# A two-line change to a block kernel on one core: the chain of each recurrence step gets the scheduler's high priority

## The chip, the cores and the metric

The kernel runs on one core of a Trainium2 chip. The time is that of one execution on the device, in microseconds (us); for the kernel before it is the median of three runs. The engines are TensorE (PE; its weight loads are shown as PEld), VectorE (DVE), ScalarE (ACT), GpSimd (POOL) and SyncE (SP), which here only issues transfers. Each engine takes its instructions in the order in which the built program holds them.

## What is computed

One block of a diffusion backbone over 2048 latent tokens and 256 context tokens of width 1024. Half of the channels go through a recurrence in 8 heads of 64, run forward and backward over context and latent tokens; the other half through a short gated convolution. Their joint output, after a projection, feeds 16 SwiGLU experts, each of which picks 256 tokens. The recurrence, per head:

```
def step(s, inp):
    r_t, w_t, k_t, v_t, a_t, b_t = inp
    sa = einsum('bhvk,bhk->bhv', s, a_t)
    s = s * w_t[:, :, None, :] + sa[..., :, None] * b_t[:, :, None, :] + v_t[..., :, None] * k_t[:, :, None, :]
    return s, einsum('bhvk,bhk->bhv', s, r_t)
```

After it: `x = x + g1 * (concat([a_x, b_x]) @ w_out)`, an RMSNorm with modulation, the router's softmax, top-k per expert, the experts, and a final RMSNorm.

## The kernel before

The program has three parts: the first projection (`proj_phase`), the recurrence with everything that is run beside it (`wkv_phase`), and the experts (`moe_phase`). The change lies in the second.

The recurrence works on chunks of C = 64 tokens: 4 of context and 32 latent, so NS = 36 steps, in each of which direction d = 0 takes a chunk from the front and d = 1 one from the back. For a step s there is preparation that needs nothing of the state: `prep` (L733, loads and scaling, for two steps at a time), `front` (L774, the 64 x 64 products, L782, masked by L784), `solve` (L806, L818 and L820: a triangular solve on DVE over two steps, with its input and output through DRAM), `merge` (L827, L839 and L843, into the one PSUM tile `pm`) and `tokmaj` (L793, transposes L798, and the load of `uv`). Then comes `chain(s)` (L846), the part that needs the state of the step before: for both directions PE forms `wy` (L857 from the state `Sb`, L860), ACT copies it to `w` (L863), PE forms `pu` (L869), ACT copies it to `uv` (L870), PE forms `ps` (L877), DVE adds it to the running state (L883) and writes the new `Sb` (two L886), POOL keeps a scaled copy (L888); PE then completes `wy` (L895). Up to step 19 a latent step's output goes to DRAM (`Y`, L899). From step TURN = 20 on the other direction has already left its half there: `chain` takes a tile `oy`, loads that half from `Y` (L850, by the helper at L57) and DVE adds `wy` to it (two L902).

`wy0` and `wy1` have one PSUM buffer each. `oy` comes from the tag `ev`, five buffers that it shares with the fill's tiles: `cu`, `cb`, `cvt` and `adacc` of the convolution and conditioning, `ccv` of the convolution's output projection, `ogg` and `ovb` of the last part.

Fill is work that PE does beside the chain: `conv_gen` (projection and convolution, 1728 of its matmuls L262 in this stage, with 256 columns), `ada_gen` (conditioning), `conv_out_gen` (L985, 16 tiles of tokens of 24 matmuls with 512 columns; loads `cx`, L998, adds with L1008, stores to `X1`, L1009), and `out_gen` (also L985, 16 tiles; normalizes `oy`, transposes with L1073, adds with L1086, router logits with L1111). All of the fill's PSUM goes through one buffer, `pj`; only for its last tiles does `out_gen` use `pg`, `pm` and others besides.

What sets the order: the program is built with a scheduler that simulates a time line. An instruction's priority is its place in the program as written; of the instructions that are ready on an engine, the one with the lowest number goes first. A tile's buffer is handed out in the same way. As the loop at L933 is written, `chain(s)` comes behind the fill of step s - 1, and `ready(s + 1)` (which calls `merge` and `tokmaj`), `scale` (which calls `prep`), `begin(s + AHEAD)` (which calls `front` and `solve`) and `fill` come behind `chain(s)`.

Of the kernel before, what the change touches and what calls it, by code (L numbers as in the profile page):

```python
# [693 lines left out]
def wkv_phase(ctx_, tc, k, I, S, fill):  # L694
    nc = tc.nc
    with ExitStack() as ctx:
# [208 lines left out]
        def begin(s):  # L905
            if s < NS:
                front(s)
                if s % 2:
                    solve(s // 2)

        def ready(s):
            if s < NS:
                merge(s)
                for d in range(2):
                    tokmaj(s, d)

        def scale(n):
            if n < NS // 2:
                for d in range(2):
                    prep(2 * n, d)  # L920
# [10 lines left out]
        begin(4)  # L931
        ready(0)
        for s in range(NS):  # L933
            chain(s)
            ready(s + 1)
            if s % 2:
                scale((s + 5) // 2)
            begin(s + AHEAD)
            fill(75 // 20 + 1 if s < TURN else 100, s >= TURN)
            if s == TURN:  # L940
                fill(0, True)


def first_half(tc, k, I, S):
    with ExitStack() as ctx:
        shared_pools(ctx, tc, k)
        fill = filler(tc, k, I, S)
        proj_phase(ctx, tc, k, I, S, fill)
        wkv_phase(ctx, tc, k, I, S, fill)
# [708 lines left out]
```

## Time and profile before

| | |
|---|---|
| median of 3 runs | 3159.18 us (3146.18 to 3162.34) |
| profiled execution: its own time | 3142.96 us |
| profiled execution: span, first to last instruction | 3141.1 us |
| PE, DVE, ACT, POOL busy | 92%, 68%, 44%, 21% of the span |
| mean granted clock of PE | 0.93 |
| first projection, recurrence, top-k and experts | 0 to 632, 632 to 1900, 1900 to 3141 us |

Times in the rows are in us from the first instruction of the profiled execution. An instruction of PE is shown with its latency; matmuls overlap, so the cost of one in a series is the distance between two starts. "Clock" is the share of TensorE's full clock that was granted.

### The profile page before, as it was taken

Reading aid. Unit: us, or ns where it says so; the run is one execution under the profiler, and the core shown is the slowest. Engines: PE = TensorE matmul, PEld = TensorE weight load, DVE = VectorE, ACT = ScalarE, POOL = GpSimd, SP = SyncE. Lnnn points to the kernel's source line nnn. Section 1 sums busy time; section 2 is a strip of 40 time slices with the busy share of each in tenths; the row PEclk is TensorE's granted clock in tenths of the full one; section 3 lists DMA queues with packets and bytes.
Section 4 is the critical chain, followed back from the end, with each engine's and each line's share of the span. In section 5 each row is a group of like instructions: output and inputs, shape, how many; then the busy total and the mean of one; then the engine's idle time right before and its main releaser. Section 6 shows DMA issues by size and latency. Waiting matters only on the chain. (4 is left out here: it accounts for less than half of the span.)

```text
span 3141.1 us, 62585 instructions
## 1 busy us (share of the span) xinstructions
PE 2881.8 (92%) x24367; PEld 2612.9 (83%) x24367; DVE 2141.5 (68%) x4611; ACT 1385.0 (44%) x2279; POOL 667.4 (21%) x893
## 2 busy tenths in 40 slices
PE   6988989889999999999999994999999999999997
PEld 4877978878888888778888873998999899999886
DVE  7688687766666666667767646666666666666776
ACT  6556645423344443224445443444444444444453
POOL 0243242533333322112222121000000000000011
PEclk8989999977999999998788986999999999999998
DMA  6466555666666655766665551666666666666886
GB/s 248 144 201 193 178 175 170 201 170 152 154 169 165 173 141 162 204 176 169 164 151 143 124 165 47 201 219 205 188 204 204 195 197 208 207 203 206 267 285 228
DMA packets 408745, 577.43 MB, mean 184 GB/s; under 512 B 175864, under 2 KB 257912, under 8 KB 407424
## 3 DMA queue, kind: packets, MB, share of 16 engines
q1 hardware_dynamic: 397504, 533.58, 56.4%
q0 software_dynamic: 10656, 38.80, 5.3%
q8 instruction: 191, 3.13, 0.4%
q10 hardware_dynamic: 288, 1.05, 0.1%
q14 instruction: 106, 0.87, 0.1%
HBM read 444.73 MB, written 128.59 MB: 183 GB/s over the span
## 5 line engine op out<-in xcount | busy, mean ns | idle before, releaser
L129 ACT CAST wH<-wr 128x1024 fp32r<-128x1024 f32 (+1 forms) x592 | 528.9, 897 | 844.7 <-PE pg L1429 408.8
L134 DVE TENSOR_TENSOR wL<-wr,wH 128x1024 fp32r<-128x1024 f32 (+1 forms) x586 | 627.6, 1076 | 353.5 <-ACT wH L129 347.6
L1429 PE MATMUL pg<-xH,wH 128*128 128x256 f32 x2048 | 585.4, 286 | 15.8 <-ACT s L1433 15.8
L1429 PE MATMUL pg<-xL,wH 128*128 128x256 f32 x2048 | 576.2, 282 | 0.0
L1429 PE MATMUL pg<-xH,wL 128*128 128x256 f32 x2048 | 575.7, 281 | 0.0
L262 PE MATMUL pj<-hH,wH 128*128 128x256 f32 x1600 | 478.0, 299 | 25.5 <-ACT cu L671 7.4
L262 PE MATMUL pj<-hH,wL 128*128 128x256 f32 x1600 | 469.4, 294 | 23.6 <-DVE wL L134 22.6
L262 PE MATMUL pj<-hL,wH 128*128 128x256 f32 x1600 | 468.1, 293 | 1.4 <-DVE hL L134 1.1
L1429 PEld LDWEIGHTS pg<-xH,wH 128*128 128x128 f32 x2048 | 389.5, 190 | 17.9 <-ACT s L1433 16.5
L1429 PEld LDWEIGHTS pg<-xL,wH 128*128 128x128 f32 x2048 | 389.3, 190 | 1.5
L1429 PEld LDWEIGHTS pg<-xH,wL 128*128 128x128 f32 x2048 | 389.5, 190 | 0.0
L262 PEld LDWEIGHTS pj<-hH,wH 128*128 128x128 f32 x1600 | 318.4, 199 | 37.6 <-DVE cu L674 8.4
L262 PEld LDWEIGHTS pj<-hH,wL 128*128 128x128 f32 x1600 | 316.6, 198 | 30.9 <-DVE wL L134 28.9
L262 PEld LDWEIGHTS pj<-hL,wH 128*128 128x128 f32 x1600 | 318.5, 199 | 5.6 <-DVE hL L134 2.0
L1488 POOL DMA_INDIRECT ACC<-o,it x30 | 50.8, 1694 | 954.4 <-DVE o L1474 800.7
L1446 PE MATMUL pd<-wH,hL 128*128 128x512 f32 x512 | 201.9, 394 | 0.0
L1446 PE MATMUL pd<-wL,hH 128*128 128x512 f32 x512 | 201.9, 394 | 0.0
L1446 PE MATMUL pd<-wH,hH 128*128 128x512 f32 x512 | 199.9, 395 | 0.0
L818 DVE TENSOR_TENSOR x<-X,x 128x120 f32<-128x120 f32 (+12 forms) x540 | 157.8, 296 | 57.7 <-DMA X<-TI 46.0
L820 DVE TENSOR_TENSOR X<-X,x 128x120 f32<-128x120 f32 (+12 forms) x540 | 163.0, 305 | 12.3
L782 PE MATMUL pg<-ar,bk 64*128 64x128 f32 x1152 | 141.0, 323 | 17.1 <-DVE g L784 7.5
L782 PEld LDWEIGHTS pg<-ar,bk 64*128 64x128 f32 x1152 | 114.4, 215 | 33.7 <-issue 13.5
(428 smaller groups left out, 5456.9 us busy)
## 6 DMA issues: line engine op xcount, KB each, us to landing
wr<-in_w_gate_dram SPq DMA_DIRECT2D x128, 512.0 KB, 4.2
wr<-in_w_up_dram SPq DMA_DIRECT2D x128, 512.0 KB, 4.8
wr<-in_w_down_dram SPq DMA_DIRECT2D x128, 512.0 KB, 3.3
wr<-in_w_in_dram SPq DMA_DIRECT2D x208, 256.0 KB, 3.2
bk<-KBD SPq DMA_DIRECT2D x36, 512.0 KB, 5.6
ar<-NR SPq DMA_DIRECT2D x36, 512.0 KB, 5.9
adaw<-in_ada_b_dram SPq DMA_DIRECT2D x32, 512.0 KB, 3.7
inc<-C SPq DMA_DIRECT2D x36, 256.0 KB, 3.1
```

Source lines behind the costliest of these rows:

```text
L129: nc.scalar.copy(H_, src)
L134: (leng or nc.vector).tensor_tensor(L_, src, H_.bitcast(F32), op=OP.subtract)
L262: nc.tensor.matmul(ps, wa[:, kw, :], ha[:, kt, :], start=m == 0, stop=m == 3 * KT - 1)
L782: nc.tensor.matmul(pg[:, p], bk[rows, p], ar[rows, p], start=True, stop=True)
L818: nc.vector.tensor_tensor(tv, X[:, 0:r, t:t + 1].to_broadcast([128, r, m]), x[:, t:t + 1, t + 1:].to_broadcast([128, r, m]), op=OP.mult)
L820: nc.vector.tensor_tensor(X[:, 0:r, t + 1:], X[:, 0:r, t + 1:], tv, op=OP.add)
L1429: nc.tensor.matmul(ps, a[:, ws], b[:, kt], start=i == 0, stop=i == 23)
L1446: nc.tensor.matmul(po[2 * m + n], a[:, f, ms], b[:, ns], start=f == 0 and q == 0, stop=f == FB - 1 and q == 2)
L1488: nc.gpsimd.indirect_dma_start(out=S["ACC"], out_offset=bass.IndirectOffsetOnAxis(ap=ids[m][:, :1], axis=0), in_=o, in_offset=None, comput ...
```

## The change

Each call of `chain` in the loop over the steps is put under the scheduler's high priority: its instructions, on every engine and its transfers too, go ahead of all others that are ready at the same time. Nothing else is edited. Lines behind L934 move by one, so L985 of before is L986 in the orders of the changed program, L1008 is L1009, and L1086 is L1087.

```
@@ -931,7 +931,8 @@
         begin(4)
         ready(0)
         for s in range(NS):
-            chain(s)
+            with tc.high_priority():
+                chain(s)
             ready(s + 1)
             if s % 2:
                 scale((s + 5) // 2)
```

On PE, between the `ps` matmuls of step 1 and the start of step 2, the order was (a row is one matmul, xN is N of them in a row; 64x64 is what is written of one head):

```order
L877 MATMUL ps<-uv,bt 64x64 x8
L843 MATMUL pm<-g,tz 32x32 x11
L782 MATMUL pg<-ar,bk 128x128 x2
L798 MATMUL pbt<-ident,bk 128x128 x4
L782 MATMUL pg<-ar,bk 128x128 x5
L798 MATMUL pbt<-ident,bk 128x128 x4
L782 MATMUL pg<-ar,bk 128x128
L857 MATMUL wy_8600<-Sb_7129,ar 128x128 x4
L860 MATMUL wy_8600<-uv,g 64x64 x8
```

and at the same place it is now

```order
L262 MATMUL pj<-hH,wH 128x256
L877 MATMUL ps<-uv,bt 64x64 x8
L262 MATMUL pj<-hL,wH 128x256
L877 MATMUL ps<-uv,bt 64x64 x8
L843 MATMUL pm<-g,tz 32x32 x16
L798 MATMUL pbt<-ident,bk 128x128 x4
L262 MATMUL pj<-hH,wL 128x256
```

The fill's matmuls (L262) now stand between the chain's; 14 of them lie between these `ps` and the next L857.

On DVE, around the adds into `oy` of step 20 (`wy_16033` and `wy_16047` are that step's two `wy`), the order was

```order
L1008 TENSOR_TENSOR cx<-pj,cx 128x512 x2
L883 TENSOR_TENSOR sc<-ps,sc 128x256
L886 TENSOR_TENSOR Sb_7129<-sc,pc 64x4x64 x2
L883 TENSOR_TENSOR sc<-ps,sc 128x256
L902 TENSOR_TENSOR oy<-wy_16033,oy 64x512
L973 TENSOR_TENSOR wo<-wo,g1row 128x512 x2
L886 TENSOR_TENSOR Sb_7130<-sc,pc 64x4x64 x2
L1008 TENSOR_TENSOR cx<-pj,cx 128x512
L902 TENSOR_TENSOR oy<-wy_16047,oy 64x512
```

and is now

```order
L836 STREAM_TRANSPOSE tz<-g 32x512
L1009 TENSOR_TENSOR cx<-pj,cx 128x512 x2
L134 TENSOR_TENSOR caL<-ccv,caH 128x512
L1009 TENSOR_TENSOR cx<-pj,cx 128x512 x2
L134 TENSOR_TENSOR caL<-ccv,caH 128x512
L1009 TENSOR_TENSOR cx<-pj,cx 128x512 x2
L134 TENSOR_TENSOR caL<-ccv,caH 128x512
L1009 TENSOR_TENSOR cx<-pj,cx 128x512
L902 TENSOR_TENSOR oy<-wy_16047,oy 64x512
L902 TENSOR_TENSOR oy<-wy_16033,oy 64x512
```

The two L902 stood beside the state update of their own step; now they stand behind the adds of the convolution's output tiles, nine of which are complete by then.

On DVE behind the last L902 of the recurrence the order held six adds L1086, of three output tiles. It now holds twelve (L1087), of six; this piece of it comes soon after that L902 and did not stand behind it before:

```order
L134 TENSOR_TENSOR oaL<-pw,oaH 128x512
L1137 SCALAR_TENSOR_TENSOR lg<-pj,or_20157,bb 64x16 x2
L1087 TENSOR_TENSOR ox<-pj,ox 128x512 x2
L1096 TENSOR_SCALAR oss<-oss 128x1
L1099 RECIPROCAL or_20434<-or_20434 128x1
L134 TENSOR_TENSOR oaL<-pw,oaH 128x512
L1137 SCALAR_TENSOR_TENSOR lg<-pj,or_20434,bb 64x16 x2
```

More of the last part's work is left for the time after the recurrence.

## Rows read from the trace of the kernel before

**Rows 1.** The page: the span, and section 1 (busy us, share, instructions) for PE.
```profile
span 3141.1 us, 62585 instructions
...
PE 2881.8 (92%) x24367; PEld 2612.9 (83%) x24367; DVE 2141.5 (68%) x4611; ACT 1385.0 (44%) x2279; POOL 667.4 (21%) x893
```
**Rows 2.** Busy time by stretch: stretch and length, engines' busy us (instructions), clock, DMA share, GB/s.
```profile
632.00:734.00 102.00, 87.21 (x730) 80.41 (x729) 73.27 (x179) 32.96 (x56) 38.42 (x53) 0.77 0.62 154
734.00:787.00 53.00, 52.47 (x483) 47.39 (x483) 30.32 (x66) 18.65 (x30) 11.70 (x17) 0.65 0.66 162
787.00:1411.00 624.00, 586.07 (x6202) 525.79 (x6200) 413.05 (x938) 229.55 (x390) 172.44 (x239) 0.96 0.62 168
1411.00:1443.00 32.00, 32.00 (x326) 26.86 (x325) 22.47 (x69) 5.58 (x9) 1.36 (x3) 1.00 0.66 180
1443.00:1707.00 264.00, 256.27 (x2541) 222.94 (x2541) 185.92 (x587) 128.77 (x247) 70.40 (x92) 0.82 0.65 157
1707.00:1855.00 148.00, 143.12 (x1610) 123.59 (x1608) 89.12 (x346) 65.84 (x143) 19.88 (x24) 0.95 0.49 117
1855.00:1900.00 45.00, 34.77 (x160) 27.41 (x159) 21.70 (x81) 20.99 (x37) 18.98 (x45) 0.79 0.72 221
```
**Rows 3.** PE's waits from 632 to 1900: us in total, times, longest.
```profile
PE pu L869 <- ACT w L863: 12.4, 6, 4.6
...
PE ps L877 <- ACT uv L870: 5.1, 3, 2.7
PE pj L985 <- DVE cx L1008: 4.9, 5, 1.6
...
PE wy L860 <- DMA uv<-V: 2.0, 1, 2.0
...
PE pj L985 <- DVE lg L1136: 1.2, 1, 1.2
```
**Rows 4.** PE in order of time from 730 to 790: start, length, what, how many.
```profile
733.60 1.06 PE L857 MATMUL wy<-Sb,ar 128*128 128x128 f32 x8
...
736.74 1.14 PE L860 MATMUL wy<-uv,g 64*64 64x64 f32 x16
...
753.48 2.07 PE L857 MATMUL wy<-Sb,ar 128*128 128x128 f32 x8
...
782.37 0.28 PE L262 MATMUL pj<-hL,wH 128*128 128x256 f32 x1
782.49 0.28 PE L262 MATMUL pj<-hH,wL 128*128 128x256 f32 x1
```
**Rows 5.** Two stretches of 20 us, with the columns of rows 2.
```profile
740.00:760.00 20.00, 20.00 (x172) 17.55 (x169) 11.48 (x20) 8.56 (x14) 8.06 (x13) 0.52 0.98 233
...
1220.00:1240.00 20.00, 20.00 (x248) 18.95 (x246) 13.01 (x20) 9.34 (x15) 3.04 (x4) 1.00 0.51 146
```
**Rows 6.** PE in order of time from 1435 to 1525, as rows 4.
```profile
1435.41 0.40 PE L985 MATMUL pj<-woH,caH 128*128 128x512 f32 x1
1435.64 0.39 PE L985 MATMUL pj<-woL,caH 128*128 128x512 f32 x1
...
1486.65 0.65 PE L1073 MATMUL pj<-ident,ox 128*128 128x128 f32 x4
...
1492.96 1.86 PE L1111 MATMUL pj<-rt,oxt 128*128 128x16 f32 x16
```
**Rows 7.** Groups by line, 632 to 1900: shapes, count | busy us, mean ns | idle before, releaser.
```profile
L886 DVE TENSOR_TENSOR Sb<-sc,pc 64x256 f32<-64x256 f32 x140 | 69.6, 497 | 1.8
...
L870 ACT COPY uv<-pu 64x512 f32<-64x512 f32 x72 | 40.9, 575 | 63.7 <-PE pu L869 63.5
...
L1008 DVE TENSOR_TENSOR cx<-pj,cx 128x512 f32<-128x512 f32 x32 | 22.0, 689 | 32.6 <-PE pj L985 25.7 <-DMA g<-TO 4.6 <-DMA cx<-in_x_dram 2.1
```
**Rows 8.** Transfers issued from 1240 to 1860: count, KB each, median us to landing.
```profile
cx<-in_x_dram SPq DMA_DIRECT2D x16, 512.0 KB, 4.2
X<-cx SPq DMA_DIRECT2D x16, 512.0 KB, 4.3
```

More of the change, by code (lines that the diff above doesn't have):

```diff
@@ L933, in wkv_phase @@
         for s in range(NS):
-            chain(s)
+            with tc.high_priority():
+                chain(s)
             ready(s + 1)
```

## Prediction, made before the changed kernel was run

> **What bounds the kernel now.** I read the page first, then a table of stretches, then TensorE's own waits, then its instructions in order of time. On the page TensorE (PE) is busy for 92% of 3141.1 us [rows 1]. The change touches one stage, the recurrence, from the first L857 at 632 us to the router's last logits at 1900 us. In the table by stretch PE is busy for 586 of 624 us, 256 of 264 and 143 of 148 there; length less busy time, added over all seven rows, is 76 of 1268 us [rows 2]. The largest wait for the chain itself, for the copy of `w`, is 12.4 us in 6 waits [rows 3]. So the recurrence isn't held up by its serial chain: PE has other work almost all the time, and moving the chain forward can't save a long wait, because there is none.
>
> What is lost here is lost to the clock. Eight matmuls of L857 take 1.06 us at 733.60 and 2.07 us at 753.48 [rows 4]: the two levels, 2.4 and 1.2 GHz. From 740 to 760 us PE is busy without a gap and the granted clock is 0.52; from 1220 to 1240 us it is just as busy at 1.00 [rows 5]. In the first stretch PE ran only the chain and its preparation (64 to 128 columns, often on part of the array); in the second it also ran L262 and L985 (256 and 512 columns, "wide" below). From [rows 2], (1 - clock) x length is 19 us for 734 to 787, 25 for 787 to 1411, 48 for 1443 to 1707 and 7 for 1707 to 1855: 98 us of PE work.
>
> **What the change moves.** Each engine gets the same instructions, but for two more loads of an activation table on ScalarE (ACT); so no work goes away, and only waits, clock and overlap can change. To see where the chain now stands I walked PE's order of both programs with full-clock rates: 0.12 us from one L262 to the next and 16 of L860 in 1.14 [rows 4], 0.23 from one L985 to the next, 4 of L1073 in 0.65 and 16 of L1111 in 1.86 [rows 6], the other small shapes likewise. (The order counts one row where the trace has two matmuls of f32.) By these rates the stage is 1006 us of PE work in either program; it takes 1268.
>
> 1. *Chain ahead of fill, steps 4 to 19.* These 16 steps held 503 us of PE work and now hold 432: fill that stood ahead of a step now stands behind it. That alone is worth **0**, since the fill still has to run before 1900.
>
> 2. *The stop at step 20.* The `oy` tile of step 20 gets a buffer only after the `ccv` tiles that share its pool. In the new order on VectorE (DVE) both L902 of step 20 stand behind the adds of L1008 for many tiles; L902 reads `wy`, which has one buffer, so L857 of step 21 can't start before. In PE's order 72 us pass between the two steps, with 20 groups of 12 L985 (ten tiles) that all go through the one `pj` buffer. Of their 19 hand-overs 8 have a block of `pm` matmuls between them and 11 have nothing. A bare hand-over costs 4.9/5 = 1.0 us [rows 3]: 11 us. The `cx` tiles have two buffers; a load of 4.2 and a store of 4.3 [rows 8] with two groups of 2.8 and two adds of 0.69 [rows 7] make 15.5 us for a buffer, 7.8 per tile against 7.2 of PE order: 6 us if only that binds, and 17 with the hand-overs on top. I take **+14**; ends 0 (all hidden) and 25 (each load also waits its turn on SP).
>
> 3. *The tail.* Behind the last L895 the order now has 14 groups of 12 L985, seven tiles, where it had 6 groups, three tiles. A tile is 24 x 0.23 + 3 x 0.65 + 1.86 = 9.3 us of PE; four more are 37 us that are merely moved. But their hand-overs through `pj` were filled by chain matmuls and now aren't. Two of the four tiles go through `pj` six times each, two (which also use `pg`) three times: 18 hand-overs. The rows for such are 1.0 (L1008) and 1.2 (the read into `lg`) [rows 3]: 18 to 22 us, less what of the next tile fits in. I take **+19**; ends 10 and 30.
>
> 4. *Shorter cover.* Between a step's last `pu` matmul and its first `ps` matmul the order now has 2.9 us of other PE work (median) where it had 3.9; between `ps` and the next L857 6.7 where it had 10.8. What must fit in is an ACT copy of 0.58 us, or on DVE an add and two products of 0.50 [rows 7]. Of the gaps ahead of `pu` and `ps` 38 were under 2.65 us, now 43; under 3.2 us 50, now 68. PE waited there 12.4 + 5.1 us in 9 waits [rows 3], some 0.4 us for each short gap; 5 to 18 more make 2 to 7 us. I take **+5**; ends 0 and 72 (the second rival below).
>
> 5. *Clock.* Wide matmuls now stand between chain matmuls more often. Stretches of PE order of 15 us and over without a wide one were 13 with 237 us, now 9 with 161; of 12 us and over, 15 with 265 us, now 15 with 239. The 98 us go with them: 0.41 us per us by the first count, 0.37 by the second, so the gain is 31 or 10 us. I take **-20**, between the two.
>
> 6. *Queues.* The chain's stores (L899) and loads of `oy` (L57) move forward on SP too, ahead of loads for the fill. PE's rows show 2.0 us for one late load of `uv` [rows 3] and no wait for weights, so these loads run ahead, and I cost it at **0**; if that cover went, a load that is late costs some 2 us each time, within the end of term 4.
>
> The sum is 14 + 19 + 5 - 20 = +18 us on the 3142.96 us of the profiled execution. That execution is 16 us under the median of the runs, 3159.18, so on the median I say **3177 us**. A measurement of this kernel can tell about 0.5%, 16 us, from no change.
>
> A rule of the skill bears on term 5. [rows 5] show half clock in 20 us in which PE had no gap. The Trainium skill, "TensorE: Matmul & The Clock Gate", section "HAM oscillation — how this bites in real kernels", ties the fall to TensorE waiting for data between bursts of matmuls. The trace disagrees with that as the whole story, since the clock was down without a wait; by that rule alone term 5 would be nothing and the sum +38.
>
> **The rivals.** *Faster by the clock.* Place: the stretches 734 to 787 and 1443 to 1707. If the mixing lifts the clock there to the 0.96 of 787 to 1411 [rows 2], 16 + 37 = 53 us come back in place of 20, and with terms 2 and 3 near their low ends (3 and 10) and term 4 at 4 the sum is 3 + 10 + 4 - 53 = -36: 3123. For it: the long stretches without wide matmuls do shrink. Against: steps 22 to 35 have some 24 to 36 L985 each, hardly more than the 24 before, and ten stretches of 11 us or more remain there. It decides from a mean clock over 0.94 in the stage up to the last step.
>
> *Chain at the head of the line.* PE takes its instructions in order. If ACT and DVE come later than the order supposes, every `pu` and `ps` group blocks the fill behind it. With a third of the 142 gaps at 1.5 us (the longest rows are 4.6 and 2.7 [rows 3]), term 4 is 72 in place of 5: 3159 + 85 = 3244. For it: the gaps are now all near their median. Against: gaps of that size rarely cost anything before.
>
> *Order is neutral.* What the stop and the tail cost, better mixing returns: 8 + 12 + 5 - 25 = 0, 3159.
>
> *The clock falls only where PE waits.* Then mixing gives nothing and terms 2 to 4 stand: +38, 3197. [rows 5] speak against it. The section of the Trainium skill named above describes this case.
>
> That the change doesn't do what it says is ruled out: the orders differ from step 0 on.
>
> **How the numbers follow.** My forecast has 0.46, of which 0.34 lies over 0.5% slower and 0.12 within; neutral 0.20; faster by the clock 0.22; head of the line 0.06; clock by waits alone 0.06. Slower by over 0.5%: 0.34 + 0.06 + 0.06 = 0.46. Within: 0.12 + 0.20 = 0.32. Faster: 0.22. The forecast's own range is 3159 to 3199 (terms 2 and 3 at 5 and 10, then at 25 and 30, the rest as taken). The whole range reaches down to 3115, which takes in most of the faster case, and up to 3225; the head of the line and the far end of the faster case, some 0.14, are left out.
>
> **What would show it.** Right: the stage is 10 to 35 us longer; a stretch of 75 to 95 us with hardly anything but L985 on PE, and waits of L985 for L1008 of 10 us or more; 90 to 110 us between the last L895 and the router's end, where it was 45; a clock over 0.82 in the steps after 21. Wrong: a clock of 0.95 throughout with a shorter stage (the first rival), or waits of PE for `w`, `uv` and `Sb` over 40 us (the second). If the part from 1900 on changes by over 5 us, something moved that I have not seen.

## The result, and the profile after

The changed kernel takes **3237.47 us** (median of 4 runs, 3231.93 to 3247.39) where the kernel before, on the same chip, takes 3152.68 (4 runs, 3142.54 to 3162.34). The ratio is 1.0286, with a 95% interval of 1.0248 to 1.0324: slower by 85 us by the medians, by 90 by the ratio. The sign was forecast, the size wasn't: 3237 lies above the range of 3115 to 3225.

The profiled execution took 3247.39 us, the longest of the four. Its page, with the span and PE's row, against [rows 1]:

```profile
span 3245.7 us, 62661 instructions
...
PE 2885.1 (89%) x24367; PEld 2616.3 (81%) x24367; DVE 2139.0 (66%) x4611; ACT 1386.2 (43%) x2281; POOL 666.7 (21%) x893
```

PE is busy for 3 us more than before, in a span that is 105 us longer. The table by stretch says where. Its columns are those of [rows 2], and the stretches hold step 0, steps 1 to 3, 4 to 19, 20, 21 to 24, 25 to 34, and step 35 up to the router's transposes:

```profile
632.00:733.00 101.00, 84.63 (x699) 78.39 (x699) 68.94 (x177) 31.54 (x53) 37.46 (x55) 0.82 0.62 157
733.00:793.00 60.00, 57.20 (x656) 51.04 (x657) 39.84 (x78) 26.00 (x43) 22.04 (x32) 0.83 0.74 187
793.00:1315.00 522.00, 478.96 (x5548) 446.33 (x5549) 352.51 (x837) 204.54 (x349) 165.06 (x224) 0.92 0.59 153
1315.00:1446.00 131.00, 112.52 (x963) 90.68 (x962) 74.93 (x196) 26.97 (x44) 5.75 (x11) 0.92 0.64 171
1446.00:1532.00 86.00, 81.31 (x814) 68.06 (x813) 50.20 (x158) 36.91 (x76) 28.00 (x34) 1.00 0.62 185
1532.00:1870.00 338.00, 289.25 (x2887) 250.27 (x2888) 204.96 (x686) 133.41 (x266) 59.89 (x77) 0.82 0.51 121
1870.00:1991.00 121.00, 88.64 (x494) 71.46 (x492) 41.95 (x136) 43.73 (x81) 18.64 (x44) 0.82 0.54 149
```

The stage ends at 1991.6 us in place of 1900.2: 91 us later. Length less busy time, added over the seven rows, is 166 us where it was 76; busy time is 1192.5 us where it was 1191.9. So **the stage's whole growth is PE standing idle**: against the same steps of before 37 us more in the row from 1532 to 1870, 23 in the last row, 18 in step 20, 10 in steps 4 to 19. What PE waited for from 632 to 1991 us, with the columns of [rows 3]:

```profile
PE pj L986 <- DVE cx L1009: 18.5, 12, 5.8
PE wy L860 <- DMA uv<-V: 14.8, 8, 6.9
PE pg L782 <- DVE g L784: 14.5, 9, 6.2
PE pj L1074 <- DVE ox L1087: 13.0, 4, 8.9
PE wy L857 <- DVE oy L902: 12.9, 3, 6.7
PE pj L986 <- DVE oaL L134: 8.1, 5, 2.3
PE pm L839 <- DVE tz L836: 8.0, 5, 2.1
PE pu L869 <- ACT w L863: 7.9, 6, 2.0
PE wy L857 <- DVE Sb L886: 7.4, 6, 1.7
PE pj L1074 <- DVE lg L1137: 7.3, 3, 4.0
...
PE wy L857 <- POOL hal L683: 2.7, 1, 2.7
```

The wait for `w`, the largest of [rows 3], fell from 12.4 to 7.9 us. In its place stand many waits of some ten us each: of the fill's matmuls for the one `pj` buffer and its readers (L1009, L1087, L1137), of L857 for the product of the step before (`oy`, `Sb`), of preparation for its inputs (`uv`, `g`, `tz`). No single new wait makes the loss: PE runs out of other work at many places.

In step 20 PE waits for L1009 for 16.1 of its 18.5 us, and DVE shows the stop of term 2, start and length in us:

```profile
1438.26 0.69 DVE L1009 TENSOR_TENSOR cx<-pj,cx 128x512 f32<-128x512 f32 x1 [3.16 <-PE pj L986]
...
1442.17 0.69 DVE L1009 TENSOR_TENSOR cx<-pj,cx 128x512 f32<-128x512 f32 x1 [2.63 <-PE pj L986]
1443.99 1.42 DVE L902 TENSOR_TENSOR oy<-wy,oy 64x512 f32<-64x512 f32 x2 [1.13 <-DMA oy<-Y]
```

L902 of step 20 comes right behind the first of the two adds of the tenth of the 16 `conv_out` tiles, when `oy` at last has a buffer and is loaded; the first L857 of step 21 starts at 1445.8.

From 1991 us to the end the profiled execution takes 13 us more than before. I had named over 5 us there as a sign of something unseen. But the thirteen other changed kernels below take 2 to 15 us more there than the one profiled execution before, those that are no slower as well; so this part isn't laid to the change.

### The profile page after: what moved, and what is told of

Read it like the earlier page. It is cut to its first block, busy times and chain, and to the rows that moved or that the text cites. A ratio compares the mean times of both kernels' runs of the same rounds, so it can differ in the third digit from the quotient of the medians.

```text
span 3245.7 us, 62661 instructions
## 1 busy us (share of the span) xinstructions
PE 2885.1 (89%) x24367; PEld 2616.3 (81%) x24367; DVE 2139.0 (66%) x4611; ACT 1386.2 (43%) x2281; POOL 666.7 (21%) x893
## 5 line engine op out<-in xcount | busy, mean ns | idle before, releaser
L262 PE MATMUL pj<-hH,wH 128*128 128x256 f32 x1600 | 475.6, 298 | 18.1 <-DVE cu L674 5.3
L262 PE MATMUL pj<-hH,wL 128*128 128x256 f32 x1600 | 467.4, 293 | 25.1 <-DVE wL L134 24.9
L262 PE MATMUL pj<-hL,wH 128*128 128x256 f32 x1600 | 466.1, 292 | 3.2 <-DVE hL L134 2.7
L262 PEld LDWEIGHTS pj<-hH,wL 128*128 128x128 f32 x1600 | 313.4, 196 | 32.9 <-DVE wL L134 30.2
L262 PEld LDWEIGHTS pj<-hH,wH 128*128 128x128 f32 x1600 | 314.6, 197 | 30.8 <-DVE cu L674 5.9
L262 PEld LDWEIGHTS pj<-hL,wH 128*128 128x128 f32 x1600 | 315.1, 197 | 8.7 <-DVE hL L134 4.1
L818 DVE TENSOR_TENSOR x<-X,x 128x120 f32<-128x120 f32 (+11 forms) x540 | 157.7, 296 | 78.8 <-DMA X<-TI 67.4
L820 DVE TENSOR_TENSOR X<-X,x 128x120 f32<-128x120 f32 (+11 forms) x540 | 159.0, 299 | 12.1
L782 PE MATMUL pg<-ar,bk 64*128 64x128 f32 x1152 | 134.1, 320 | 16.9 <-DVE g L784 14.5
```

The lines of the kernel that those rows point to most:

```text
L262: nc.tensor.matmul(ps, wa[:, kw, :], ha[:, kt, :], start=m == 0, stop=m == 3 * KT - 1)
L782: nc.tensor.matmul(pg[:, p], bk[rows, p], ar[rows, p], start=True, stop=True)
L818: nc.vector.tensor_tensor(tv, X[:, 0:r, t:t + 1].to_broadcast([128, r, m]), x[:, t:t + 1, t + 1:].to_broadcast([128, r, m]), op=OP.mult)
L820: nc.vector.tensor_tensor(X[:, 0:r, t + 1:], X[:, 0:r, t + 1:], tv, op=OP.add)
```

## The experiments

The words "stage" and "idle" mean in all of them: from the first L857 to the router's transposes in the profiled execution, and the time in it in which PE does nothing. "Lead" is how far the chain runs ahead of the wide work that was written before it; PE's order gives it as the number of wide L986 done when a step begins. The ratios are against runs of the kernel before on the same chip.

### Which steps cost: high priority early, late, and with oy apart

**early_only.** `with tc.high_priority() if s < TURN else ExitStack():` (an empty `ExitStack` does nothing)

> High priority for the chains of steps 0 to 19 alone; those of steps 20 to 35 at the ordinary one. Theory A (from step 20 on a chain that runs ahead keeps an oy tile, one of the five ev buffers, longer, so that the loads of oy, ogg and ovb wait for one another and PE with them): the slow steps 25 to 31 and the long tail go, the time is 3140 to 3175. Theory B (it is the order alone that costs, pauses and tail without cover, buffers have no part in it): the same, 3140 to 3175. Theory C (steps 0 to 19 cost, because they push wide work behind step 20, which then lies there without cover): the loss stays, 3205 to 3240.

**late_only.** The same line with `s >= TURN`.

> High priority for the chains of steps 20 to 35 alone. Theory A: most of the loss of the changed kernel is here, 3200 to 3235, with steps 25 to 31 at over 33 us each. Theory B: the tail alone is longer by some 25 us, and the steps by their lost cover, 3175 to 3215. Theory C: no loss, 3140 to 3165.

**oy_own2.**

```
-  k.y[s] = k.bp.tile([128, H, C], F32, name="oy", tag="ev", bufs=5)
+  k.y[s] = sb.tile([128, H, C], F32, name="oy", bufs=2)
-  sc = sb.tile([128, HP, C], F32, name="sc", bufs=4)
+  sc = sb.tile([128, HP, C], F32, name="sc", bufs=3)
```

> The changed kernel with the oy tiles in two buffers of their own in the recurrence's pool (the tile sc has three buffers in place of four, to make room). Theory A: the stop of some 18 us in step 20 and the slow steps 25 to 31 (37 us of idle time, and the clock lost with it) go, the tail shrinks as well: 3150 to 3190. Theory B: buffers have no part, only the stop in step 20 goes: 3210 to 3240. Theory C: 3205 to 3240.

**early_oy_own2.** Both edits.

> Both edits together: high priority in steps 0 to 19 alone, and the oy tiles in two buffers of their own. Theory A: no worse than either alone, 3130 to 3165. Theory B: as high priority in steps 0 to 19 alone, within 10 us of it. Theory C: 3205 to 3240.

Measured: 1.0114 (1.0079 to 1.0150), 1.0115 (1.0079 to 1.0152), 1.0223 (1.0188 to 1.0258) and 1.0129 (1.0081 to 1.0177), about +36, +36, +70 and +41 us. Idle PE by steps, in us:

| steps | before | changed | early_only | late_only | oy_own2 | early_oy_own2 | oy_own5 (below) |
|---|---|---|---|---|---|---|---|
| 0 to 3 | 21 | 18 | 18 | 29 | 18 | 18 | 21 |
| 4 to 19 | 33 | 43 | 43 | 29 | 43 | 42 | 42 |
| 20 | 0 | 18 | 12 | 0 | 3 | 0 | 8 |
| 21 to 24 | 1 | 5 | 6 | 14 | 37 | 33 | 6 |
| 25 to 34 | 11 | 48 | 13 | 20 | 28 | 19 | 35 |
| 35 to the router | 10 | 33 | 16 | 23 | 12 | 8 | 29 |
| stage | 76 | 166 | 109 | 115 | 141 | 121 | 140 |

Either half of the change costs 36 us, so A (most of it late) and C (all of it early) fall as they were put; by the ratios the two halves make 72 of the 90. B comes nearest: the medians of all four (3175.6, 3175.0, 3212.0 and 3177.5) lie in its ranges or within 1 us of them. But for oy_own2 it had the stop in step 20 simply go, and it moved. What high priority costs early is paid mainly in steps 4 to 20, what it costs late in steps 21 to 35. Only in steps 25 to 34 do they strengthen each other: 2 and 8 us more than before when alone, 37 together.

In oy_own2 step 20 is short (40 us), and step 22 takes 157, with the same wait:

```profile
PE pj L986 <- DVE cx L1009: 14.6, 15, 4.3
PE pm L839 <- DVE tz L836: 5.4, 1, 5.4
```

The stop has moved by two steps. So it isn't the sharing of `ev` alone that makes it. With two buffers of its own the chain can go two steps further, and then it stops for an `oy` buffer all the same.

### How far the chain may run: five oy buffers, and a high priority with an offset

**oy_own5.** As oy_own2 with `bufs=5` for `oy`, and `bufs=1` for the solver's `x` and `X`.

> The changed kernel with five buffers of their own for the oy tiles, in the recurrence's pool; to make room sc has three buffers in place of four, and the solver's x and X one each in place of two. Theory D (it is how far the chain may run ahead of the wide work that counts: the number of free oy buffers says at which step the conv_out groups are run off in one stretch without cover, and what is put off there is missing as cover to the end): the long step moves from step 20 (oy among five shared buffers) and step 22 (two of its own) to step 25, the idle time of PE in the stage stays over 125 us against 76 of before, and the time is 3195 to 3235. Theory A (the waits for buffers themselves are the loss, so that enough buffers end it): no step over 50 us, 3150 to 3185.

**off100, off300.** `with tc.high_priority(100):`, and 300.

> The high priority of the chain with an offset of 100 in place of none, so that the chain passes only what was written shortly ahead of it. By the order of instructions PE has then 300 of the 384 conv_out matmuls done at the start of step 20 (before 324, changed 0) and 20 groups more of the out tiles at the start of step 35 than the changed kernel. Theory D: the loss goes with the lead, 3135 to 3165. A theory that the high priority costs by itself, whatever the lead (head of line on DVE and ACT, loads moved past others on SP): 3180 to 3215.

> The same with an offset of 300: 240 of the 384 conv_out matmuls at the start of step 20. Theory D: between off100 and the changed kernel and nearer to off100, 3145 to 3180. High priority by itself: as off100 to within 10 us, 3180 to 3215.

Measured: oy_own5 1.0189 (1.0131 to 1.0246), off100 1.0114 (1.0078 to 1.0151), off300 1.0041 (1.0013 to 1.0070).

oy_own5 came out as theory D had it. The long step is now step 25, the stage's idle time 140 us. The row is the stretch of that step, with the columns of [rows 2]; below it PE's longest wait there:

```profile
1505.00:1586.00 81.00, 63.98 (x542) 50.54 (x541) 58.75 (x162) 19.26 (x35) 14.73 (x22) 0.85 0.64 179
```

```profile
PE pj L986 <- DVE cx L1009: 8.6, 2, 7.8
```

Steps 20, 22, 25: the place of the stop goes with the number of buffers that `oy` can have, and most of the loss stays (1.0223 and 1.0189 for 1.0286). Part of theory A holds all the same: in steps 26 to 34 PE is idle for 44 us in the changed kernel, for 20 with two buffers of `oy`'s own and 18 with five, before 11. (Of the 35 us in the table 17 are the stop of step 25.) What the buffers taken from `sc`, `x` and `X` cost was not measured by itself.

**It is the lead that costs**: with less of it, in off100 and off300, the idle time is 76 and 85 us. Whatever wide work the chain passes must run later, when there is less of the chain left to run beside it. In the changed kernel 600 L986 are done when step 35 begins, before 672, in oy_own5 588; the tail is idle for 33, 10 and 29 us. In oy_own2 684 are done, and the tail is idle for 12.

off100 (median 3187) missed D's range and lies in that of the other theory; off300 (3164) lies in D's and not in the other's. That high priority costs by itself, through waits, off100 doesn't show: its idle time is 76 us, just that of before, and its tail is shorter (49 us for 70); yet its stage is 36 us longer, all of it *busy* PE. The same matmuls take longer. PE in order of time shows how:

```profile
808.22 0.39 PE L262 MATMUL pj<-hL,wH 128*128 128x256 f32 x1
808.53 0.33 PE L877 MATMUL ps<-uv,bt 128*64 128x64 f32 x2
808.79 0.38 PE L262 MATMUL pj<-hH,wL 128*128 128x256 f32 x1
809.11 0.33 PE L877 MATMUL ps<-uv,bt 128*64 128x64 f32 x2
...
810.16 0.28 PE L262 MATMUL pj<-hH,wL 128*128 128x256 f32 x1
810.28 0.28 PE L262 MATMUL pj<-hH,wH 128*128 128x256 f32 x1
```

An L262 and an L877 in turn come round every 0.57 us (808.22 to 808.79). In a row an L262 comes every 0.12 us, and an L877 (two records, one matmul of fp32) takes some 0.06. With the small offset the chain passes the fill by a little and is then woven into it matmul by matmul: in the trace there are 444 changes between the wide matmuls (L262 and L986, rounded fp32) and all others in the stage, before 258, changed 296, off300 298. (The expectations below count them in the program's order, which gives some ten more.)

### What a change of kind costs, and short leads

**probe.** The kernel before, with a block of matmuls ahead of everything that uses only a matrix of ones on the diagonal (`k.identr` is rounded fp32, `k.ident` the same read as fp32):

```
wide  = lambda: nc.tensor.matmul(a, k.identr, m, start=True, stop=True)                      # 256 columns
thin  = lambda: nc.tensor.matmul(b, k.ident[:, 0:64], k.ident[:, 0:64], start=True, stop=True)
thinr = lambda: nc.tensor.matmul(b, k.identr[:, 0:64], m[:, 0:64], start=True, stop=True)
```

> The kernel before with a block of matmuls ahead of everything, which uses no other data: 96 wide ones (128x256, rounded fp32) in a row, 96 narrow ones (64x64, fp32) in a row, the two kinds in turn one by one, four by four, and wide ones in turn with narrow ones of the rounded type. Theory E (a change of kind costs): a pair in turn takes 0.25 us and more beyond the sum of the two in rows, four by four about a quarter of that for each matmul pair. Rival (in off100 something else of the stage made L262 longer after narrow matmuls): a pair in turn costs the sum. The block itself adds some 150 to 250 us to the time.

PE in order of time, start and length; L1564 is `wide`, L1565 `thin`, L1566 `thinr`:

```profile
25.09 10.13 PE L1565 MATMUL b<-ident 128*64 128x64 f32 x170
35.15 11.69 PE L1564 MATMUL a<-m,ident 128*128 128x256 f32 x97
46.77 0.33 PE L1565 MATMUL b<-ident 128*64 128x64 f32 x2
47.03 0.39 PE L1564 MATMUL a<-m,ident 128*128 128x256 f32 x1
47.34 0.33 PE L1565 MATMUL b<-ident 128*64 128x64 f32 x2
...
142.01 0.68 PE L1565 MATMUL b<-ident 128*64 128x64 f32 x8
142.62 0.74 PE L1564 MATMUL a<-m,ident 128*128 128x256 f32 x4
143.29 0.68 PE L1565 MATMUL b<-ident 128*64 128x64 f32 x8
...
182.28 0.19 PE L1566 MATMUL b<-m,ident 128*64 128x64 f32 x1
182.31 0.36 PE L1564 MATMUL a<-m,ident 128*128 128x256 f32 x1
182.51 0.20 PE L1566 MATMUL b<-m,ident 128*64 128x64 f32 x1
```

In rows a wide one takes 0.12 us (11.69/97) and a thin one 0.12 (10.13/85): 0.24 for a pair. In turn a pair takes 0.57 (46.77 to 47.34), 0.33 more. Four by four they take 1.28 (142.01 to 143.29) for 0.96, 0.32 more. So two changes cost **0.32 us**, whether one matmul lies between them or four. The clock is 1.00 in all of these rows. With a thin matmul of the rounded type a pair takes 0.23 us, which leaves 0.11 for the thin one and both changes together; a row of these alone was not run. The rival falls.

**late30, late100.** `with tc.high_priority(30) if s >= TURN else ExitStack():`, and 100. **early500.** `(500) if s < TURN`.

> High priority with an offset of 30, and in steps 20 to 35 alone. Steps 0 to 19 are then those of before, conv_out has 324 of its 384 matmuls done at the start of step 20 as there, the out tiles stand two tiles further at the start of step 35 (720 matmuls of L985 for 672), and PE changes 272 times between wide and narrow matmuls, as often as before (268). Theory E (the lead costs PE idle time, and every change between the wide matmuls and the narrow ones costs some 0.15 us, so that a short lead with as few changes costs nothing): 3125 to 3155, at or below before. A theory that the high priority costs by itself: over 3160.

> The same with an offset of 100: 270 changes, 696 matmuls of L985 at the start of step 35; steps 20 to 35 as in off100, where they took some 490 us as in before. Theory E: 3130 to 3160. High priority by itself: over 3160.

> High priority with an offset of 500 in steps 0 to 19 alone: conv_out has 180 of 384 matmuls done at the start of step 20, 282 changes. Theory E: as high priority in steps 0 to 19 with no offset, with a shorter stop in step 20: 3145 to 3170, PE idle in the stage 85 to 100 us. If only the changes mattered and not the lead: 3140 to 3150, idle as before (76).

Measured: late30 **1.0263** (1.0229 to 1.0298), late100 1.0059 (1.0033 to 1.0085), early500 1.0014 (0.9990 to 1.0038). early500 came out as theory E had it, with 91 us of idle time. late100 (median 3170) and late30 (3231) did not; both lie where the other theory put them. late30 is the plainest miss, since its idle time (74 us) and its changes between wide and narrow are those of before; busy PE grew by 78 us. Here the narrow ones are woven into each other:

```profile
1447.51 0.33 PE L877 MATMUL ps<-uv,bt 128*64 128x64 f32 x2
1447.77 0.24 PE L843 MATMUL pm<-g,tz 32*32 32x32 f32 x2
1447.94 0.33 PE L877 MATMUL ps<-uv,bt 128*64 128x64 f32 x2
1448.20 0.24 PE L843 MATMUL pm<-g,tz 32*32 32x32 f32 x2
```

Both are fp32, but L877 uses 128 x 64 of the array and L843 32 x 32. A pair comes round in 0.43 us, where each alone in a row takes some 0.06: again 0.3 for two changes. The Trainium skill, "TensorEngine Tiling (Array Packing)", section "Tiling Modes", says that changing the tiling mode drains TensorE; the price in these rows agrees. The probe's rounded pair, 128 x 64 and 128 x 128 in turn, with at most 0.11 us for the narrow matmul and both changes, shows that not every such change costs as much.

So the count to look at is that of all changes from one line's matmuls to another's on PE, in the stage's trace:

| kernel | ratio | stage | idle | busy | (1 - clock) x length | changes |
|---|---|---|---|---|---|---|
| before | 1 | 1268 | 76 | 1192 | 129 | 994 |
| changed | 1.0286 | 1359 | 166 | 1193 | 161 | 805 |
| off100 | 1.0114 | 1304 | 76 | 1229 | 132 | 1244 |
| off300 | 1.0041 | 1290 | 85 | 1205 | 128 | 1051 |
| late30 | 1.0263 | 1344 | 74 | 1270 | 163 | 1344 |
| late100 | 1.0059 | 1294 | 83 | 1210 | 149 | 1047 |
| early500 | 1.0014 | 1269 | 91 | 1178 | 126 | 939 |
| lt4_500 (below) | 0.9959 | 1245 | 72 | 1174 | 112 | 1004 |

With 0.125 us for a change and the clock's loss in full, busy time comes out within 10 us in all rows (late30: 350 x 0.125 + 34 = 78, measured 78; off100: 250 x 0.125 + 3 = 34, measured 37). That is a sum fitted to these rows, an estimate, not a measurement of each part; for the seven changed kernels that are not in the table it comes out within 12 us. By it the changed kernel's busy time stayed the same because 189 changes fewer (-24) met 32 us more of lost clock. Each row is one execution. In the run probe, whose recurrence is that of before in nearly the same order (348 L985 done when step 20 begins, for 324), the stage is idle for 86 us and busy for 1179, and loses 120 by the clock; differences of some ten us in the table mean nothing. High priority by itself isn't what costs: early500, and lt4 below, have it in their early steps and take as long as before (1.0014 and 0.9978).

### Is there a gain in the first steps?

**lt4.** `with tc.high_priority() if s < 4 else ExitStack():` **lt4_500.** `(500) if s < 4`. **lt8_500.** `(500) if s < 8`.

> High priority for the chains of steps 0 to 3 alone. By the order of instructions the rest is as before: conv_out at 324 of 384 at the start of step 20, 696 matmuls of L985 at the start of step 35 (before 672), 268 changes between wide and narrow matmuls (268). Theory F (the lead in the first steps gains what term 5 of the prediction said, some 12 to 18 us of clock, and the loss is made where the put-off wide work must be run off without cover, in step 20 and behind it): 3125 to 3145, faster than before or the same. Theory G (the gain in the first steps is only wide work put off, and comes back in the steps that follow): 3140 to 3165, with steps 4 to 19 longer by what steps 0 to 3 are shorter.

> The same with an offset of 500: 348 of 384 at the start of step 20, 684 at step 35, 258 changes between wide and narrow. Theory F: 3120 to 3145. Theory G: 3135 to 3160.

> High priority with an offset of 500 for the chains of steps 0 to 7 alone: 204 of 384 at the start of step 20, 648 at step 35, 270 changes. Theory F: the put-off work is partly worked off by step 20, 3130 to 3155, with PE idle in the tail between before (10 us) and early500 (18 us). Theory G: 3140 to 3165.

Measured: lt4 0.9978 (0.9954 to 1.0002), lt4_500 **0.9959** (0.9931 to 0.9987), lt8_500 1.0043 (1.0021 to 1.0064). lt4_500 is faster than both kernels, by some 13 us on that of before. Its stretches of steps 0, 1 to 3, 4 to 19, and 35, with the columns of [rows 2], and below them steps 1 to 3, 4 to 19, and 35 of before:

```profile
633.00:734.00 101.00, 86.89 (x701) 80.30 (x702) 70.78 (x176) 31.39 (x53) 38.06 (x53) 0.79 0.62 153
734.00:796.00 62.00, 56.76 (x666) 50.77 (x666) 41.75 (x83) 27.06 (x45) 22.70 (x33) 0.85 0.71 184
796.00:1413.00 617.00, 586.98 (x6086) 527.21 (x6086) 405.11 (x928) 221.31 (x377) 168.62 (x227) 0.95 0.63 169
...
1824.00:1878.00 54.00, 46.05 (x342) 39.01 (x340) 26.32 (x120) 28.66 (x52) 19.38 (x45) 0.92 0.68 204
```

```profile
733.60:826.90 93.30, 87.47 (x850) 79.95 (x849) 64.12 (x166) 31.18 (x53) 21.44 (x37) 0.76 0.62 153
826.90:1410.90 584.00, 551.37 (x5838) 493.56 (x5836) 379.55 (x839) 217.41 (x368) 163.02 (x219) 0.97 0.63 170
...
1830.50:1900.20 69.70, 59.27 (x378) 48.77 (x377) 31.67 (x129) 31.75 (x58) 19.71 (x47) 0.81 0.63 183
```

Steps 1 to 3 take 62 us for 93, steps 4 to 19 617 for 584: what is put off comes back in full by the end of step 19, as theory G has it. It comes back without idle time (30 us in steps 4 to 19, before 33); 16 steps of chain are left to run it beside. In lt4, too, steps 0 to 3 are 24 us shorter and steps 4 to 19 20 longer. So the rows show no lasting gain in the first steps, and theory F's reason is not borne out. What lt4_500 gains stands behind step 19, most of it in step 35 (54 us for 70); why is not shown. Its profiled execution (3124.5 us) is 12 us under the median of its runs, so the rows flatter it, and that median, 3136, lies in the ranges of both theories. lt8_500, with 204 of 384 L986 by step 20, is slower again, by 14 us; its profiled execution was the fastest of its twelve runs, and doesn't show where.

## Why the prediction was wrong

**The sum.** Terms 2, 3 and 4 added 38 us of idle PE; measured are 90. Term 5 gave back 20; measured is nothing. Of the 73 us by which the stage's growth (91) passes the sum (18), idle PE outside step 20 and the tail makes 44 (49 measured, 5 taken), term 5 makes 21, terms 2 and 3 make 8.

**Term 5, the clock, is a step that failed by its sign.** The loss by the clock grew from 129 to 161 us in place of falling by 20. Long stretches without wide matmuls did become fewer, and in steps 0 to 3 the loss fell from 46 to 28 us. By steps, (1 - clock) x length in us:

| steps | 0 to 3 | 4 to 19 | 20 | 21 to 24 | 25 to 34 | 35 to the router |
|---|---|---|---|---|---|---|
| before | 46 | 19 | 0 | 24 | 27 | 13 |
| changed | 28 | 39 | 10 | 0 | 61 | 22 |

It grew in the steps in which PE's idle time grew by ten us and more. The row of steps 25 to 34 before, against that from 1532 to 1870 above (clock 0.90, then 0.82):

```profile
1557.40:1830.50 273.10, 261.65 (x2833) 227.85 (x2833) 178.02 (x616) 128.61 (x263) 59.47 (x74) 0.90 0.58 139
```

I took "wide work stands between the chain's matmuls" to be enough for the full clock. In the probe PE alternates wide and narrow matmuls without a gap, and most of that runs at half the clock (last section), so it isn't always enough. What lost the clock in the changed kernel stays open. Against the mixing: off100 changes between wide and narrow half as often again (444 times for 296) and loses 132 us. Against the waits alone: late30 is idle for 74 us and loses 163. I had also priced each matmul as it runs in a row, by full-clock rates; the 189 changes that the new order saves weren't in the sum, nor any price for them. (The row of 740 to 760 us in [rows 5] also holds 8 small L205, and that of 1220 to 1240 no L985, which first runs at 1242; the sum doesn't use either.)

**Term 4, idle PE in the steps themselves, is the step that failed by its size, and terms 1 and 6 with it.** Term 1 put steps 4 to 19 at 0 since the fill "still has to run before 1900": their idle time grew by 10 us (42 to 43 us in all five kernels with high priority there and no offset, 28 to 35 in the four with none), and 12.1 us there are waits for a late `uv`, which term 6 put at 0. Term 4 looked only at the gaps ahead of `pu` and `ps`, and there waits fell from 17.5 us to 10.3 where it added 5. But idle time in steps 21 to 34 grew from 13 to 53 us, in waits that had no term: L857 for `oy` (12.9 us), the out tiles' matmuls for their own copies and adds (some 18), `pm` for `tz` (6.3). My "end" of 72 us for term 4 would have held it, for another reason.

What I missed in steps 21 to 34 is that the lead is limited by the buffers of `oy`. Once it is used up, the chain goes at the pace at which the out tiles free them, and little else is left for PE beside those two. The runs show that the buffers set the place of the stop (steps 20, 22, 25) and that early and late lead strengthen each other in steps 25 to 34 (2 and 8 us alone, 37 together). With buffers of `oy`'s own the idle time of steps 26 to 34 falls from 44 us to 20 and 18, and with five L857 waits for `oy` for 1.9 us in steps 25 to 34 in place of 12.9. So most of it goes with those buffers; the time saved is only 20 to 30 us by the ratios, with the stop in a later step. What makes the rest, over the 11 us of before, isn't shown.

**Term 2, the stop at step 20**, was right: 18 us of idle time for 14, by the wait named (L986 for the adds, 16.1 us), at the step named; the stretch of little but L986 is 98 us long (1348 to 1446) where 75 to 95 was named. **Term 3, the tail**, was near: 23 us more idle time for 19; from the last L895 to the router 113 us, just over the 90 to 110 that was named. **Term 6** put the queues at 0; waits for a late `uv` grew from 2.0 to 14.8 us, so it was too low by some 13. Why the loads come late isn't shown. A sign was badly chosen: the clock in steps 21 to 34 is 0.85, over the 0.82 named, but it was 0.87 before.

**The rivals.** "Head of the line" gave 3244, near to what came, but not by its mechanism: waits for `w`, `uv` and `Sb` are 18 us (33 with the late loads of `uv`), not over 40. "The clock falls only where PE waits" gave 3197; the probe, where the profile shows no wait, speaks against the "only". "Faster by the clock" wanted 0.95; the stage has 0.88, before 0.90. "Order is neutral" had mixing return what the stop and the tail cost; busy PE is as before, 1192 us.

## What to carry to other kernels

High priority for a serial chain makes no work go away; where the profile shows that the chain hardly waits, without a limit it only used up the work that would have covered the chain later. Before moving a chain forward, count what is left to run beside its last steps, and which buffer ends its lead. And count in the order of TensorE's instructions how often the kind of matmul changes: an order woven more finely can cost as much as a stop (late30: 78 us, the clock's greater loss included), in time that the profile calls busy.

## What the runs showed of the hardware

**A change of matmul kind on TensorE costs some 0.16 us**: from rounded fp32 to fp32 and back 0.32 to 0.33 us for the two changes in the probe, and 0.3 us between two fp32 kinds on differently shaped parts of the array (late30), all at a clock of 1.00. PE is shown as busy meanwhile. Not every change costs this: the probe's rounded pair has at most 0.11 us for two.

**The clock can fall to half while the profile shows TensorE busy without a gap.** In the probe PE alternates one wide and one narrow matmul from 46.8 to 127 us. A stretch of it, and the four-by-four stretch, with the columns of [rows 2]:

```profile
60.00:126.00 66.00, 66.00 (x216) 41.40 (x216) 0.00 (x0) 0.00 (x0) 0.00 (x0) 0.50 0.00 0
141.00:170.00 29.00, 29.00 (x276) 24.48 (x273) 0.00 (x0) 0.00 (x0) 0.00 (x0) 1.00 0.01 2
```

In the first it is busy for 66.00 of 66 us at a clock of 0.50 (1.2 GHz). Four by four, with the same matmuls, the clock is 1.00 (2.4 GHz). Over half of a pair one by one is the price of the two changes (0.33 of 0.57 us), four by four a quarter (0.32 of 1.28); whether TensorE works in that time isn't shown. The Trainium skill, "TensorE: Matmul & The Clock Gate", section "HAM oscillation — how this bites in real kernels", ties such a fall to TensorE waiting between bursts; here it happens without a wait that the profile shows.
